# Sample attention in two visits a sample instead of three: the outputs are turned with the next sample's weights

## The chip, the cores and the metric

The kernel runs on one core of a Trainium2 chip. The metric is the device time of one execution in microseconds (us). The version before takes 2600.63 us, the median of 3 runs (2598.29 to 2601.8 us). One execution of it was profiled; it took 2600.23 us, and its span from the first to the last recorded instruction is 2598.4 us.

Engines are named as in the profile: PE is TensorE (matrix multiplications and transposes), PEld its weight loads, DVE is VectorE, ACT is ScalarE, POOL is GpSimd, SP is the engine whose queue issues most of the transfers. Each engine works through its own list of instructions in a fixed order; an instruction that waits holds up all that stand behind it in the same list.

## The reference

One inference step of a two-layer encoder over 512 prompt tokens and 8 running streams ("samples") of 16 new tokens, which share all weights. For each layer:

```
x += 1/2 * SwiGLU_1(RMSNorm(x))
z  = RMSNorm(x) @ w_in            # conv B | C | V | q | k | v | gates
y_c = B * causal_conv3(C * V)
y_a = attention(q, k, v)          # 8 heads of 64
m  = sigmoid(g_c) * (y_c @ w_conv_out) + sigmoid(g_a) * (y_a @ w_attn_out)
x += m @ w_o
x += 1/2 * SwiGLU_2(RMSNorm(x))
```

For a sample the attention has 16 queries, and 256 cached plus 16 new keys and values:

```
s   = q @ k_all.T / 8 + bias      # 8 heads x 16 queries = 128 rows, 272 columns
p   = softmax(s)
y_a = p @ v_all                   # a sum over 272 keys, for each head
```

Everything is computed in 32-bit floats; the large products are made of three matmuls with operands that are split into a high and a low part.

## The kernel before

All activations lie transposed, as tiles of 128 features by 640 tokens (512 of the prompt, then 16 for each sample). Weights come from memory in 384 blocks of 128 x 1024, issued from SP (`load`, line 204) into three buffers `raw`. ACT rounds each block to a high part `whi` (line 264), DVE subtracts it to get the low part `wlo` (line 269), each with three buffers; PE multiplies both.

The mixer's projections q, k, C, V, B and the gates are computed two output tiles at a time by `seven` (line 664): 14 *steps*, each a `block` (line 345) of six matmuls 128 x 320 into the PSUM tiles `ma`, `mb`, `mc`, with copies of partial sums (`capsm` and `c`, lines 681, 688, 691) between them. `others` and `qk` string these steps together into one `stream` of 140 steps a layer. `attention` (line 1103) interleaves the attention with it: `fill(n)` takes the next `n` steps of the stream, so that PE has something to do while ACT and DVE work on the softmax. The prompt's four pairs of heads take 68 of the steps, the eight samples the other 72, which are all that is left. What `fill` asks for beyond them gives PE nothing: only what follows the last step's matmuls on DVE and ACT is still put out then. The last steps of the stream are the first pair of gate tiles `g`, whose sigmoids (line 881) follow on ACT.

PE goes through its work in the order of the program (`manual_schedule(engines={PE})`, line 948). The order of DVE, ACT, POOL and SP within this part is set by a scheduler when the program is built, and the program then keeps to it. After `attention`, in `outputs` (line 1017), PE, DVE and ACT all follow the program's order. Its first work is `gate_pair(2)`, whose first matmuls go into the PSUM tile `qa`.

A sample `b` goes through these stages:

- `sscores(b)` (line 1257) issues the transfers of its cached keys (`kc`), cached values (`vc`) and new values (`vn`) from SP, and has POOL copy the new keys behind the cached ones. Four matmuls on PE make the scores `spss`; DVE adds the bias and writes them to a wide tile `ss` (called `box`), DVE and ACT make the softmax in it, without the division.
- `svalues(b)`, first part: PE turns the weights with three transposes (`sptp`, lines 1295 and 1296); ACT copies two of the results to `pt` (line 1298) and DVE the third to `pn` (line 1299), both further columns of the same `box`.
- second part: twelve matmuls make the outputs `spy` (line 1306); ACT scales them by the reciprocal of the sum and writes them to `yx` (line 1308), again columns of `box`.
- third part: PE turns `yx` with one transpose into its quarter of the PSUM tile `ptx` (line 1312), which four samples share. After the fourth, DVE and ACT copy `ptx` to `yas` (line 1317), which `outputs` reads later.

A *visit* is a place where PE leaves the stream for a sample. In the loop at line 1323 a sample has three: the weights' transposes; then the scores of sample `b + 2` with the outputs of sample `b`; then the output's transpose. With `fill` around them that is 4 steps, visit, 3 steps, visit, 2 steps, visit. PSUM has four banks for the tiles `spss`, `sptp`, `spy` and `ptx` (tag `att`), of which `ptx` holds one over four samples; the tiles of `outputs` take the same four banks after them. `box`, `vn` and `vc` have two buffers each (tags `pt`, `bias` and `s`), so what belongs to sample `b + 2` can be written only when the last reader of sample `b` is done.

## Time and profile before

| | before |
|---|---|
| median of 3 runs | 2600.63 us (2598.29 to 2601.8) |
| profiled execution | 2600.23 us |
| its span | 2598.4 us |
| PE busy | 2568.8 us, 99% |
| DVE busy | 1952.8 us, 75% |
| ACT busy | 1119.0 us, 43% |
| the sample section of the first layer | about 592 to 673 us of the span |
| the sample section of the second layer | about 1876 to 1956 us of the span |
| in 592 to 674 us: PE, DVE, ACT busy | 82.00, 65.22 and 40.30 of 82.00 us |
| one matmul 128 x 320 behind another | about 0.147 us from start to start |

Between the first and the last recorded instruction lie 2598.4 us; 1.8 us of the profiled execution lie around that. A row of a list in order of time has the start, the duration (of several instructions that are merged: from the first's start to the last's end), the engine, the line of the kernel, the operation, and what it writes and reads; "x8" says that eight instructions are merged, and a bracket at the end tells idle time before and what ended it. Matmuls overlap: one of 0.31 us starts 0.147 us after the one before it, so their cost is read from the distances of their starts. The fp32 matmuls of the samples stand twice in the records, a transpose once.

### The profile page before, as it was taken

The page shows a single profiled execution, that of the slowest core. Times are in us where ns is not written, and L with a number is a line of the kernel's source. Part 1 is how long each engine was busy: PE and PEld are TensorE (multiplying, and loading weights), DVE is VectorE, ACT ScalarE, POOL GpSimd, SP SyncE. Part 2 cuts the span into 40 slices and gives each one's busy share as a digit, 9 for nine tenths or more (in the row PEclk, how much of TensorE's full clock was granted, in tenths as well). Part 3 has the DMA queues.
Part 4 walks back from the last instruction along what each step waited for, and adds up shares of the span by engine and source line. Part 5 has one row for each costly group of instructions (what it writes and reads, how often), then busy time and mean ns, then how long its engine had stood idle before and what let it go on. Part 6 is the DMA issues. An engine that isn't in the chain of part 4 may idle for free.

```text
span 2598.4 us, 42553 instructions
## 1 busy us (share of the span) xinstructions
PE 2568.8 (99%) x17576; PEld 2506.6 (96%) x17576; DVE 1952.8 (75%) x3037; ACT 1119.0 (43%) x1738; POOL 59.6 (2%) x153
## 2 busy tenths in 40 slices
PE   8999999999999999999999999999999999999998
PEld 8999999888999999999999999998899999999998
DVE  7687768678777987767787767686876778877676
ACT  5343335454444543334454333355544445433332
POOL 0000000111000000000000000001110000000000
PEclk9999999999999999999999999999999999999999
DMA  3232222225222232222222222222342222222222
GB/s 132 72 106 84 74 90 98 98 88 165 97 74 90 67 104 82 73 90 81 82 82 98 74 90 82 76 98 101 119 145 89 82 82 79 91 91 74 87 90 76
DMA packets 74066, 237.06 MB, mean 91 GB/s; under 512 B 8240, under 2 KB 19120, under 8 KB 73872
## 3 DMA queue, kind: packets, MB, share of 16 engines
q1 hardware_dynamic: 70272, 223.90, 25.7%
q0 software_dynamic: 2880, 9.79, 1.1%
q8 instruction: 138, 2.26, 0.4%
q10 hardware_dynamic: 720, 0.65, 0.1%
q14 instruction: 56, 0.46, 0.1%
HBM read 225.85 MB, written 7.94 MB: 90 GB/s over the span
## 4 chain that ended last, share of the span: by engine, by line
PE 90%; DVE 6%; ACT 2%; issue 1%; DMA 1%; POOL 0%; SPq 0%; ACTq 0%; DVEq 0%; POOLq 0%
PE pab L351 12%; PE pda L337 11%; PE pdb L337 11%; PE paa L351 11%; PE pcb L351 6%; PE pca L351 5%; PE py L337 4%; PE po L337 4%; PE qa L351 4%; PE pbb L351 3%; PE pba L351 3%; PE pv L1156 2%; PE qc L351 2%; PE ma_cv L351 2%; DVE wlo L269 1%; PE ma_b L351 1%
## 5 line engine op out<-in xcount | busy, mean ns | idle before, releaser
L269 DVE TENSOR_TENSOR wlo<-raw,whi 128x1024 fp32r<-128x1024 f32 (+2 forms) x540 | 562.3, 1046 | 178.1 <-ACT whi L264 177.8
L264 ACT CAST whi<-raw 128x1024 fp32r<-128x1024 f32 (+2 forms) x540 | 490.4, 912 | 264.6 <-PE pca L351 79.4
L351 PE MATMUL pab<-xhib,whi 128*128 128x320 f32 x704 | 218.4, 310 | 0.4 <-ACT u_b L788 0.4
L351 PE MATMUL pab<-xlob,whi 128*128 128x320 f32 x704 | 217.5, 309 | 0.0
L351 PE MATMUL pab<-xhib,wlo 128*128 128x320 f32 x704 | 217.5, 309 | 0.0
L351 PE MATMUL paa<-xhia,whi 128*128 128x320 f32 x640 | 198.2, 310 | 0.7 <-ACT c_a L724 0.5
L351 PE MATMUL paa<-xloa,whi 128*128 128x320 f32 x640 | 197.7, 309 | 0.0
L351 PE MATMUL paa<-xhia,wlo 128*128 128x320 f32 x640 | 197.7, 309 | 0.0
L337 PE MATMUL pda<-ahia,whi 128*128 128x320 f32 x704 | 160.5, 309 | 0.6 <-DVE x L854 0.6
L337 PE MATMUL pda<-aloa,whi 128*128 128x320 f32 x704 | 160.5, 309 | 0.0
L337 PE MATMUL pda<-ahia,wlo 128*128 128x320 f32 x704 | 160.3, 309 | 0.0
L264 ACT CAST whi<-s 128x1024 fp32r<-128x1024 f32 (+1 forms) x120 | 109.5, 912 | 111.3 <-DVE s L208 89.5
L337 PE MATMUL pdb<-alob,whi 128*128 128x320 f32 x656 | 149.5, 309 | 0.0
L337 PE MATMUL pdb<-ahib,wlo 128*128 128x320 f32 x656 | 149.5, 309 | 0.0
L337 PE MATMUL pdb<-ahib,whi 128*128 128x320 f32 x656 | 149.3, 309 | 0.0
L269 DVE TENSOR_TENSOR wlo<-s,whi 128x1024 fp32r<-128x1024 f32 (+1 forms) x120 | 127.0, 1058 | 9.7 <-ACT whi L264 9.7
L351 PEld LDWEIGHTS pab<-xhib,whi 128*128 128x128 f32 x704 | 132.1, 188 | 1.2 <-ACT u_b L788 0.9
L351 PEld LDWEIGHTS pab<-xlob,whi 128*128 128x128 f32 x704 | 132.2, 188 | 0.2
L351 PEld LDWEIGHTS pab<-xhib,wlo 128*128 128x128 f32 x704 | 132.1, 188 | 0.0
L351 PEld LDWEIGHTS paa<-xhia,whi 128*128 128x128 f32 x640 | 120.2, 188 | 1.3 <-ACT c_a L724 0.8
L351 PEld LDWEIGHTS paa<-xloa,whi 128*128 128x128 f32 x640 | 120.2, 188 | 0.1
L351 PEld LDWEIGHTS paa<-xhia,wlo 128*128 128x128 f32 x640 | 120.2, 188 | 0.0
(576 smaller groups left out, 6965.0 us busy)
## 6 DMA issues: line engine op xcount, KB each, us to landing
raw<-in_wst SPq DMA_DIRECT2D x384, 512.0 KB, 3.5
kc<-in_kcache SPq DMA_DIRECT2D x32, 256.0 KB, 4.0
vc<-in_vcache SPq DMA_DIRECT2D x16, 512.0 KB, 4.6
bias<-in_pbias POOLq DMA_DIRECT2D x16, 256.0 KB, 3.1
x<-in_xin SPq DMA_DIRECT2D x8, 320.0 KB, 5.1
out_vo<-v POOLq DMA_DIRECT2D x10, 256.0 KB, 2.5
out_ko<-k POOLq DMA_DIRECT2D x8, 320.0 KB, 2.4
out_yout<-x SPq DMA_DIRECT2D x8, 192.0 KB, 1.9
```

The costliest lines, as they stand in the source:

```text
L264: ACT.copy(hi[:, d], src[:, c])
L269: DVE.tensor_tensor(out=lo, in0=src, in1=hi.bitcast(F32), op=ALU.subtract)
L337: PE.matmul(ps[:, a, :HT], w, x[:, a * HT : (a + 1) * HT], start=k == 0 and j == 0, stop=k == n - 1 and j == 2)
L351: PE.matmul(ps, a, b, start=start and kp == 0 and j == 0, stop=stop and kp == NP - 1 and j == 2, skip_group_check=True)
L1156: PE.matmul(pv[t], xx[:, t * P : (t + 1) * P], w[:, kk * AW : (kk + 1) * AW], start=c == 0 and kk == 0 and j == 0, stop=c == KT // 2 - 1 a ...
```

## The change

The output of sample `b` is no longer turned in a visit of its own. It waits until sample `b + 1` comes to the transposes of its weights, and is turned just ahead of them, in the same visit. A sample then has two visits: 5 steps of the stream, visit (one transpose for the sample before, three for this one), 4 steps, visit (scores of sample `b + 2`, outputs of sample `b`). The number of steps for a sample stays 9, and the instructions are the same; their places differ. The last sample's output has no next sample: it is turned behind the loop, after a `fill(2)`.

As `yx` now has to outlive the scores of sample `b + 2`, which take the buffer of `box`, it moves from `box` to the first 128 columns of the tile of the new values `vn`, which the output matmuls have read by then. That tile is allocated with all 128 rows in place of 16. `vn` of sample `b + 2` can now be loaded only when the output of sample `b` has been turned.

```diff
             rows = slice(b * TS, (b + 1) * TS)
-            vn = mp.tile([P, SEQ], F32, name=f"vn{n}", tag="bias")[:TS, :AW]
-            SP.dma_start(vn, vnew[rows])
+
+            vn = mp.tile([P, SEQ], F32, name=f"vn{n}", tag="bias")
+            SP.dma_start(vn[:TS, :AW], vnew[rows])
...
             pt = box[:, KS : KS + 2 * P].rearrange("p (a b) -> p a b", a=2)
-            pn, yx = (box[:n, KS + o * P : KS + (o + 1) * P] for n, o in ((TS, 2), (P, 3)))
+            pn = box[:TS, KS + 2 * P : KS + 3 * P]
+            yx, vn = vn[:, :P], vn[:TS]
...
         sscores(0)
         sscores(1)
+
+        vals = None
         for b in range(NB):
+            fill(5)
+            if vals:
+                next(vals, None)
             vals = svalues(b)
+            next(vals)
             fill(4)
-            next(vals)
-            fill(3)
             if b + 2 < NB:
                 sscores(b + 2)
             next(vals)
-            fill(2)
-            next(vals, None)
+        fill(2)
+        next(vals, None)
         fill(KT * KT)
```

## Prediction

> **What bounds the kernel now.** I read the page first (busy shares, chain), then the list of who waited for whom on PE, then the section in order of time on PE and ACT, then the granted clock by stretches.

> ```profile
> PE 2568.8 (99%) x17576; PEld 2506.6 (96%) x17576; DVE 1952.8 (75%) x3037; ACT 1119.0 (43%) x1738; POOL 59.6 (2%) x153
> ...
> PE 90%; DVE 6%; ACT 2%; issue 1%; DMA 1%; POOL 0%; SPq 0%; ACTq 0%; DVEq 0%; POOLq 0%
> ```

> PE is busy nearly all the time and carries 90% of the chain. A microsecond in which PE stands still is a microsecond of the kernel.

> ```profile
> PE ptp L1221 <- DVE s L1344: 10.1, 6, 2.3
> ...
> PE qa L351 <- ACT capsm L1043: 0.5, 2, 0.2
> ```

> PE's longest waits in the middle of the kernel are in the prompt's attention (ptp, up to 2.3 us). Asked for the sample section alone, this list is empty: PE waits there for nothing, so there is no wait that the change could remove. Just behind it, at line 1043 in each layer, comes a wait of 0.2 us.

> ```profile
> 666.40 0.31 PE L351 MATMUL ma_g<-tlo,whi 128*128 128x320 f32 x1
> 666.55 0.31 PE L351 MATMUL ma_g<-thi,wlo 128*128 128x320 f32 x1
> 666.70 0.38 PE L1295 MATMUL sptp<-ident,ss 128*128 128x128 f32 x2
> 666.91 0.27 PE L1296 MATMUL sptp<-ident,ss 128*16 128x128 f32 x1
> 666.94 0.39 PE L351 MATMUL ma_g<-thi,whi 128*128 128x320 f32 x1
> 667.17 0.31 PE L351 MATMUL ma_g<-tlo,whi 128*128 128x320 f32 x1
> ...
> 669.76 0.42 PE L1306 MATMUL spy<-vn,ss 16*32 16x128 f32 x8
> ...
> 672.41 0.31 PE L351 MATMUL ma_g<-thi,wlo 128*128 128x320 f32 x1
> 672.55 0.27 PE L1312 MATMUL ptx<-ident,ss 128*128 128x128 f32 x1
> 672.58 0.39 PE L351 MATMUL qa<-hhim,whi 128*128 128x320 f32 x1
> 672.81 0.31 PE L351 MATMUL qa<-hlom,whi 128*128 128x320 f32 x1
> ```

> This is the last sample of the first layer. The visit for the weights takes 666.55 to 667.17, 0.62 us, where two matmuls of the stream would take 0.29: 0.33 us for three transposes, 0.11 each. The visit for the output takes 672.41 to 672.81, 0.40 us against 0.29: 0.11 us for one. So a transpose costs the same alone or in company, and going to a visit costs nothing of its own.

> ```profile
> 671.04 0.36 ACT L1308 ACTIVATE ss<-spy,sst 128x128 f32<-128x128 f32 x1
> 671.43 0.62 ACT L264 CAST whi<-raw 128x512 fp32r<-128x512 f32 x1
> 672.08 1.28 ACT L881 ACT_TABLE_LOAD   x1
> 673.37 1.55 ACT L881 ACTIVATE g<-g,sm 128x640 f32<-128x640 f32 x2
> 674.94 0.37 ACT L1317 COPY ya<-ptx 64x256 f32<-64x256 f32 x1
> ```

> Same place on ACT: the last sample's scaling stands ahead of the table load and the two sigmoids of the gates, the copy of the turned outputs behind them.

> **The change part by part**, against the profiled execution's own 2600.23 us (0.4 below the median of the runs).

> *The visit that goes.* Eight samples, two layers: 16 transposes move from 0.11 us alone to 0.11 us in company. Taken from finer starts it is 0.003 us each, a gain of 0.05 us in all. Ends: 0 and 16 x 0.11 = 1.8, if the fourth transpose were free; the row of three at 0.11 each speaks for nearly 0.

> *More cover between the stages.* Weights' copies to output matmuls: 4 steps in place of 3 (one step is 0.88 us, half of "12 matmuls in 1.76"). Nothing waits there now, so this is worth 0.

> *The last sample, the costly part.* All 72 steps are used up when the loop ends, so the `fill(2)` behind it gives PE nothing, and the last transpose follows the last output matmuls directly. Those move behind the two steps that followed them: from 669.76 to 671.5, and PE comes to the transpose at about 672.45. But in the changed program's order of instructions the last scaling on ACT stands behind the weight cast, the table load and the first of the two sigmoids. By the rows above the first sigmoid begins at 673.37, the next instruction 0.74 later at 674.11; the scaling takes 0.36, so the transpose starts at 674.5: PE stands for 2.05 us. Then `qa`. Because `ptx` for samples 4 to 7 is now allocated after `spy` of sample 4, it gets the PSUM bank in which `qa` comes next (before, another), and the program's first `qa` matmul waits for ACT's copy of the turned outputs. ACT has the second sigmoid ahead of it (674.4, 0.74 apart), then the copy, 0.37: 675.5. `qa` began at 672.58, so 2.94 us later. The second layer has the same rows 1283.6 us later (table load at 1955.67): another 2.94. If ACT's list were no obstacle, the scaling alone (about 0.4 with its 0.28 us matmul latency ahead) would still be exposed: lower end about 0.7 a layer; upper end, both sigmoids and the copy one after another after 673.37, 3.2.

> *Behind it.* The wait at line 1043 (0.24 us at 680.12; the starts there are 0.55 apart instead of 0.15, so 0.40) comes from ACT being late with copies; ACT's list starts only 2.2 us later there and PE 2.9, so it goes: -0.40 a layer.

> *A new small wait in the first sample.* Behind its scaling the changed order on ACT has the cast of the next weights, the exponential of sample 2, then the partial sum `c`. PE's block that has to wait for this copy would start at 605.8. The cast can begin when the step before has been read, about 604.1, 0.95; exponential 0.52; copy 0.41: 606.0, and a restarted PE loses another 0.1 between the first two matmuls. 0.25 a layer (ends 0 and 0.4). I find no second place of this kind: elsewhere the copies are ready 0.3 us or more ahead.

> *SP.* `vn` now waits for the transpose of sample b, five steps later than the output matmuls, and the weight blocks stand behind it in SP's list. The tightest: one issued at 648.26 now stands behind a `vn` whose transpose comes at about 648.0 and whose issue takes 0.61: about 648.9, 0.6 late; what is made of it is needed 1.4 us or more after it is ready. 0, because of that cover; if none of the 16 were covered, 16 x 0.6 = 10.

> *The four copies to `yas`* move one visit on; DVE and ACT have room (65 and 40 of 82 us). 0.

> Sum a layer: 2.94 + 0.25 - 0.40 = 2.8, twice 5.6: **2605.8 us with PE at full clock.**

> *The clock after the stall.*

> ```profile
> 503.70:507.10 3.40, 2.98 (x21) 2.63 (x19) 3.40 (x9) 1.61 (x5) 1.22 (x3) 1.00 0.17 69
> 507.30:510.60 3.30, 1.52 (x8) 1.02 (x9) 3.24 (x9) 0.48 (x2) 0.00 (x0) 1.00 0.01 2
> 510.70:514.00 3.30, 3.30 (x15) 3.30 (x14) 1.77 (x2) 1.58 (x3) 0.00 (x0) 0.50 0.00 0
> 514.10:517.40 3.30, 3.30 (x24) 2.67 (x24) 1.61 (x4) 1.52 (x4) 0.00 (x0) 1.00 0.54 179
> ```

> The columns are the stretch, its length, PE busy with its count, PEld, DVE, ACT, POOL, then the granted clock. After a stretch with PE busy for 1.52 of 3.3 us (the 2.33 us wait at ptp) the clock is 0.50 for 3.4 us; the matmuls start 0.265 us apart instead of 0.147. That holds 13 instead of 23 and loses up to 1.5 us. It happens four times, after both such waits of each layer. The new stall is 2.9 us idle of 3.1. If a 3.4 us stretch holds most of it, the clock halves; if the boundary falls in its middle, perhaps not. I take 1.3 each (part of the half clock falls into the stall): 2605.8 + 2.6 = **2608.4 us**; ends 0 and 3.0.

> [...]

> **The rivals.**

> [...]

> *Not slower: `qa` does not wait for the copy.* If the stall ends with the transpose, as it would were the bank read out in time by the DVE half alone, a layer costs 2.05 + 0.25 - 0.40 = 1.9 and, with so much less idle time, no clock: 2604.0. It decides as soon as a layer loses under 2.6 us. Against: the program's wait is for ACT's half.

> *SP's list becomes the bound*: weight blocks come too late in the section. Where the 0.6 us delays exceed their cover in half the places, 16 x 0.6 / 2 = 5 on top: 2613. Against: the cover of 1.4 us.

> *Faster*: visits have a cost that the starts don't show. It would have to be over 0.35 us each, 16 times, to pay for the stall alone; the rows leave 0.003.

> **How the numbers follow.** Clock halved in both layers 0.42 (2608.4), in one 0.22 (2607.1), in none 0.17 (2605.8), no wait for the bank or a shorter stall 0.08 (2604.0), SP 0.08 (2613), faster 0.03. I predict 2608.4. The range 2604.5 to 2610.5 leaves out SP, faster and half of the short stall. A measurement of this kernel tells about 0.2%, 5.2 us, from no change: the border is 2605.8. Slower: nearly all of the first two, half of the third, SP: 0.78. Faster 0.03, within 0.19.

> **What would show it.** In the profile after: PE waiting about 2.05 us at ptx for ACT's line 1308 and 0.7 to 0.9 at `qa` for the copy to `ya`, once a layer; no waits elsewhere in the section except some 0.2 us at `mc_b` in the first sample; the wait at line 1043 gone; two more stretches of 0.50 clock behind `qa`. I am wrong if PE does not wait at the last ptx, if weight casts make it wait in mid-section, or if the clock stays at 1.00 behind `qa`.

## The result and the profile after

The changed kernel takes 2608.71 us, the median of 6 executions (2604.18 to 2611.66), beside 2600.22 us of the kernel before (6 executions, 2598.29 to 2601.8) on the same chip. The ratio is 1.0032, with a 95% interval of 1.0021 to 1.0044: slower. The profiled execution has a span of 2606.9 us, 8.5 us more than before.

The first view is again the list of who waited for whom on PE, in the kernel after (total us, times, longest us):

```profile
PE ptp L1221 <- DVE s L1350: 10.1, 6, 2.3
...
PE ptx L1314 <- ACT vn L1310: 3.8, 2, 1.9
PE qa L351 <- ACT ya L1319: 1.8, 2, 0.9
```

The prompt's waits at ptp are what they were. Two lines are new, once a layer each: PE waits 1.9 us at the last ptx for ACT's scaling, and 0.9 us at qa for ACT's copy to `ya`. The line of `capsm` at 1043 has left the list. Asked for the sample section without its end (590 to 672 us), the list is empty, as it was.

The end of the first layer's sample section in order of time, on PE:

```profile
671.36 0.42 PE L1308 MATMUL spy<-vn,ss 16*32 16x128 f32 x8
671.71 0.65 PE L1308 MATMUL spy<-vc,ss 128*32 128x128 f32 x16
674.24 0.33 PE L1314 MATMUL ptx<-ident,vn 128*128 128x128 f32 x1 [1.89 <-ACT vn L1310]
675.48 0.41 PE L351 MATMUL qa<-hhim,whi 128*128 128x320 f32 x1 [0.91 <-ACT ya L1319]
```

and the same stretch on ACT:

```profile
671.81 1.28 ACT L881 ACT_TABLE_LOAD   x1
673.11 0.83 ACT L881 ACTIVATE g<-g,sm 128x640 f32<-128x640 f32 x1
673.84 0.35 ACT L1310 ACTIVATE vn<-spy,sst 128x128 f32<-128x128 f32 x1
674.09 0.82 ACT L881 ACTIVATE g<-g,sm 128x640 f32<-128x640 f32 x1
675.06 0.37 ACT L1319 COPY ya<-ptx 64x256 f32<-64x256 f32 x1 [0.15 <-DVE ya L1319]
```

The outputs `spy` are done near 672.4, but ACT is in a table load and then in the first sigmoid; its scaling (line 1310) starts at 673.84, and PE follows at 674.24. The copy to `ya` starts at 675.06, and `qa` at 675.48. The bracket of the copy says that DVE's half of it ended last, 0.15 us after the second sigmoid.

Where the 8.5 us lie is read by setting the starts of the same matmuls in the two traces side by side, at places where both have the same visits behind them:

| what moves PE in the profiled execution | first layer | second layer |
|---|---|---|
| `mc_b` in the first sample | +0.37 | +0.37 |
| start of `qa`, from there | +3.00 | +3.03 |
| half clock behind `qa` | +1.55 | +1.39 |
| the wait at line 1043 and the restart behind it | -0.50 | -0.51 |
| sum | +4.42 | +4.28 |

At line 1043 the first matmul gains 0.41 and 0.42 us; the rest lies in the distance to the one behind it, which is 0.25 us after the wait and 0.15 without it. The table adds up to 8.7 us. The remaining -0.2 us are scattered: around the prompt's waits the first layer is 0.7 us faster than before and the second, which has one half-clock stretch more, 0.6 us slower; small drifts elsewhere make up the rest.

The granted clock behind the two stalls, by stretches of 3.41 us (length, busy time with count of PE, PEld, DVE, ACT and POOL, granted clock, DMA share, GB/s):

```profile
673.49:676.90 3.41, 1.75 (x10) 1.56 (x11) 1.01 (x2) 1.78 (x4) 0.00 (x0) 1.00 0.02 5
676.90:680.31 3.41, 3.41 (x15) 3.41 (x14) 0.91 (x1) 2.31 (x4) 0.00 (x0) 0.50 0.01 2
1960.31:1963.72 3.41, 0.96 (x21) 0.50 (x17) 2.78 (x6) 3.23 (x6) 0.00 (x0) 1.00 0.00 0
1963.72:1967.13 3.41, 3.05 (x11) 3.06 (x12) 0.00 (x0) 0.30 (x1) 0.00 (x0) 0.50 0.00 0
```

In both layers the stretch that follows runs at 0.50. The small wait in the first sample is seen on PE and on ACT:

```profile
605.16 0.31 PE L351 MATMUL ma_b<-thi,wlo 128*128 128x320 f32 x1
605.56 0.42 PE L351 MATMUL mc_b<-hhim,whi 128*128 128x320 f32 x1
605.82 0.31 PE L351 MATMUL mc_b<-hlom,whi 128*128 128x320 f32 x1
```

```profile
603.64 1.05 ACT L264 CAST whi<-raw 128x1024 fp32r<-128x1024 f32 x1 [0.57 <-PE mc_b L351]
604.59 0.52 ACT L1346 ACTIVATE ss<-ss,sst 128x272 f32<-128x272 f32 x1
...
605.11 0.40 ACT L691 COPY c<-mc_b 128x320 f32<-128x320 f32 x1
```

The block starts 0.40 us after the matmul before it, in place of 0.147, when the copy to `c` ends, which had the weight cast and sample 2's exponential ahead of it on ACT: 0.25 us. Its second matmul comes 0.26 later, another 0.11.

### The profile page after: what moved, and what is told of

Same layout as the page of the kernel before. It is cut to its first block, busy times and chain, and to the rows that moved or that the text cites. A ratio compares the mean times of both kernels' runs of the same rounds, so it can differ in the third digit from the quotient of the medians.

```text
span 2606.9 us, 42568 instructions
## 1 busy us (share of the span) xinstructions
PE 2572.3 (99%) x17576; PEld 2510.6 (96%) x17576; DVE 1953.2 (75%) x3037; ACT 1120.2 (43%) x1738; POOL 54.1 (2%) x153
## 4 chain that ended last, share of the span: by engine, by line
PE 90%; DVE 6%; ACT 2%; issue 1%; DMA 0%; POOL 0%; DVEq 0%; ACTq 0%; POOLq 0%
PE pab L351 12%; PE pda L337 11%; PE pdb L337 11%; PE paa L351 11%; PE pcb L351 6%; PE pca L351 5%; PE py L337 4%; PE po L337 4%; PE qa L351 4%; PE pbb L351 3%; PE pba L351 3%; PE pv L1156 2%; PE qc L351 2%; PE ma_cv L351 2%; DVE wlo L269 1%; PE mc_cv L351 1%
## 5 line engine op out<-in xcount | busy, mean ns | idle before, releaser
L264 ACT CAST whi<-raw 128x1024 fp32r<-128x1024 f32 (+2 forms) x540 | 490.7, 912 | 271.4 <-PE pca L351 79.4
L351 PE MATMUL pab<-xhib,whi 128*128 128x320 f32 x704 | 218.4, 310 | 0.4 <-ACT u_b L788 0.4
L351 PE MATMUL pab<-xlob,whi 128*128 128x320 f32 x704 | 217.5, 309 | 0.0
L351 PE MATMUL pab<-xhib,wlo 128*128 128x320 f32 x704 | 217.5, 309 | 0.0
L351 PE MATMUL paa<-xhia,whi 128*128 128x320 f32 x640 | 198.2, 310 | 0.7 <-ACT c_a L724 0.5
L351 PE MATMUL paa<-xloa,whi 128*128 128x320 f32 x640 | 197.6, 309 | 0.0
L351 PE MATMUL paa<-xhia,wlo 128*128 128x320 f32 x640 | 197.6, 309 | 0.0
L264 ACT CAST whi<-s 128x1024 fp32r<-128x1024 f32 (+1 forms) x120 | 109.5, 913 | 98.6 <-DVE s L208 80.6
L351 PEld LDWEIGHTS pab<-xhib,whi 128*128 128x128 f32 x704 | 132.1, 188 | 1.2 <-ACT u_b L788 0.9
L351 PEld LDWEIGHTS pab<-xlob,whi 128*128 128x128 f32 x704 | 132.2, 188 | 0.2
L351 PEld LDWEIGHTS pab<-xhib,wlo 128*128 128x128 f32 x704 | 132.1, 188 | 0.0
L351 PEld LDWEIGHTS paa<-xhia,whi 128*128 128x128 f32 x640 | 120.2, 188 | 1.3 <-ACT c_a L724 0.8
L351 PEld LDWEIGHTS paa<-xloa,whi 128*128 128x128 f32 x640 | 120.2, 188 | 0.1
L351 PEld LDWEIGHTS paa<-xhia,wlo 128*128 128x128 f32 x640 | 120.2, 188 | 0.0
```

The source lines that it names most:

```text
L264: ACT.copy(hi[:, d], src[:, c])
L351: PE.matmul(ps, a, b, start=start and kp == 0 and j == 0, stop=stop and kp == NP - 1 and j == 2, skip_group_check=True)
```

## The experiments

Times are medians, compared with executions of the kernel before on the same chip (medians 2600.03 to 2600.46 us). The theory under test: the loss is the end of the sample section (the missing steps in front of the last transpose, ACT's order, the PSUM bank) and the half clock behind it; the rest of the change costs nothing but 0.37 us a layer.

### Another bank for ptx

```diff
-            if vals:
-                next(vals, None)
-            vals = svalues(b)
-            next(vals)
+            old, vals = vals, svalues(b)
+            for v in (vals, old) if b == G + 1 else (old, vals):
+                if v:
+                    next(v, None)
```

> The changed kernel, with the PSUM bank of ptx for samples 4 to 7 and that of sptp for sample 5 exchanged (in one visit the weights are turned ahead of the outputs), so that qa gets a bank that was read out long ago; before 2600.2 us, changed 2608.7 us. If the wait of 0.91 us at qa comes from the bank alone, it goes in both layers and the wait of 1.9 us at ptx stays: 2606.9 us if the clock still halves behind the shorter stall, 2603.9 us if it does not. If qa waits for something else than the bank, nothing changes: 2608.7 us.

Measured: 2604.72 us, ratio 1.0019 (1.0009 to 1.0028). PE at the end of the first layer's section:

```profile
673.01 0.33 PE L1314 MATMUL ptx<-ident,vn 128*128 128x128 f32 x1 [1.89 <-ACT vn L1310]
673.09 0.39 PE L351 MATMUL qa<-hhim,whi 128*128 128x320 f32 x1
```

`qa` follows ptx at once: the 0.91 us are the bank's, in both layers, and the 1.89 us at ptx stay. In the profiled execution the clock is not halved behind either stall:

```profile
668.86:672.27 3.41, 2.25 (x34) 1.59 (x32) 3.41 (x8) 2.93 (x4) 0.00 (x0) 1.00 0.00 0
672.27:675.68 3.41, 2.67 (x19) 2.67 (x20) 0.99 (x2) 2.26 (x6) 0.00 (x0) 1.00 0.02 5
675.69:679.10 3.41, 3.41 (x25) 3.41 (x25) 2.50 (x3) 3.41 (x6) 0.00 (x0) 1.00 0.12 22
```

Here the idle time is split over two stretches. The execution that was profiled took 2600.32 us, which is less than the 2603.9 expected for a full clock and about what the kernel before takes, although both stalls are in it. Its prompt part explains that: there the trace has two half-clock stretches where the kernel before has four, and the starts show the two prompt parts 1.9 us and 1.8 us shorter. So the clock behind the prompt's waits differs from one trace to another too, and this profile is that of one of the fastest executions. The median lies between the two times expected for a full and a halved clock. Single executions spread from 2600.14 to 2608.39 us, at a mean granted clock of 0.997 in those below 2601 and 0.993 to 0.994 in the two above 2608.

### Two steps kept for the end

```diff
-            fill(5)
+            fill(5 - (b == NB - 1))
             if vals:
                 next(vals, None)
             vals = svalues(b)
             next(vals)
-            fill(4)
+            fill(4 - (b == NB - 1))
```

> The changed kernel, with one step taken from each of the last sample's two fills, so that the fill(2) behind the loop has two steps to give; the bank stays that of the changed kernel. My theory: the wait at ptx goes, since the scaling comes ahead of the table load on ACT again, but the copy to ya stays behind both sigmoids, and qa waits for it from about 672.3 to 675.4 instead: the whole stall moves to qa, about 2.8 us a layer, the clock halves as before, and the time is 2608.5 us (2606.5 to 2610). The rival, that the missing steps at ptx are the loss and the bank is only a detail on top: 2602 us or less.

Measured: 2607.92 us, ratio 1.0029 (1.0018 to 1.0041). The wait at ptx is gone, and the list of waits on PE has in its place:

```profile
PE qa L351 <- ACT ya L1319: 4.9, 2, 2.4
```

On ACT the scaling now comes ahead of the table load, and the copy still behind both sigmoids:

```profile
672.59 0.36 ACT L1310 ACTIVATE vn<-spy,sst 128x128 f32<-128x128 f32 x1
...
673.62 1.28 ACT L881 ACT_TABLE_LOAD   x1
674.92 1.55 ACT L881 ACTIVATE g<-g,sm 128x640 f32<-128x640 f32 x2
676.49 0.37 ACT L1319 COPY ya<-ptx 64x256 f32<-64x256 f32 x1
```

By the starts, with what the section had lost before taken off, `qa` comes 2.66 us later than before in each layer, where the theory had 2.8. With both causes it is 3.0 us, with the stall at ptx alone (the experiment above) 1.9. So each cause alone brings most of the delay, and they overlap. The rival, with 2602 us or less, falls.

The clock did not quite do as expected: in the profiled execution it is halved behind the wait in the second layer only.

```profile
672.40:675.81 3.41, 2.08 (x16) 1.80 (x13) 3.29 (x7) 3.35 (x6) 0.00 (x0) 1.00 0.00 0
675.82:679.23 3.41, 2.32 (x16) 2.32 (x17) 0.60 (x2) 1.22 (x3) 0.00 (x0) 1.00 0.02 5
1959.20:1962.61 3.41, 0.98 (x8) 0.71 (x6) 2.76 (x6) 3.27 (x5) 0.00 (x0) 1.00 0.00 0
1962.61:1966.02 3.41, 3.41 (x13) 3.41 (x14) 0.00 (x0) 0.00 (x0) 0.00 (x0) 0.50 0.00 0
```

In the first layer the idle time is split over two stretches. That this execution still took 2607.91 us is in part a coincidence: its trace is 1.4 us behind that of the kernel before from the first 11 us of the kernel on, far from the edit.

### Both edits together

The edits of the last two, in one kernel.

```diff
-            fill(5)
-            if vals:
-                next(vals, None)
-            vals = svalues(b)
-            next(vals)
-            fill(4)
+            fill(5 - (b == NB - 1))
+            old, vals = vals, svalues(b)
+            for v in (vals, old) if b == G + 1 else (old, vals):
+                if v:
+                    next(v, None)
+            fill(4 - (b == NB - 1))
```

> Both of the last two edits: two visits a sample, two steps behind the last outputs, and another bank for ptx. My theory: no stall at ptx, none at qa, no halved clock behind them, the wait of 0.2 us at line 1043 back; the rest of the change (visits in company, yx in the buffer of vn, later loads of vn on SP) costs nothing but the 0.37 us at mc_b in each layer's first sample: 2600.9 us (2600 to 2602). The rival, that merged visits or the delayed loads cost something in the section: over 2603 us. The rival that a visit has a price of its own: under 2599.5 us.

Measured: 2600.65 us, ratio 1.0003 (0.9995 to 1.0012). No wait is left at ptx or at qa:

```profile
672.22 0.27 PE L1314 MATMUL ptx<-ident,vn 128*128 128x128 f32 x1
672.25 0.39 PE L351 MATMUL qa<-hhim,whi 128*128 128x320 f32 x1
```

This kernel has two visits a sample, `yx` in the buffer of `vn`, and the later loads, and it is as fast as before; the interval leaves at most 3 us for all of that. Of the changes only the 0.37 us at `mc_b` are left in its trace, in each layer, and 0.1 us less at line 1043. The slowest of its 11 executions took 2602.25 us; that speaks against the rival of the delayed loads at over 2603 us; a price of 0.35 us for each visit, 5.6 us in all, would have shown as a gain.

### The stall alone, in the kernel before

```diff
         for b in range(NB):
             vals = svalues(b)
-            fill(4)
+            fill(4 + (b == NB - 1))
             next(vals)
-            fill(3)
+            fill(3 + (b == NB - 1))
```

> The kernel before, three visits a sample, yx in box, with nothing changed but the last sample: one step more in each of its first two fills, so that its fill(2) has none left. Of the change this is the last sample's missing cover alone, without the bank. My theory: ACT's order becomes that of the changed kernel (scaling behind the table load and the first sigmoid), PE waits 1.9 us at ptx and not at qa; qa 2.0 us later, 0.4 us less at line 1043, so 3.2 us in two layers: 2603.4 us with a full clock, 2606.3 us with the clock halved in both layers. The rival, that the loss comes from the visits or from yx in vn: 2600.2 us.

Measured: 2606.61 us, ratio 1.0028 (1.0017 to 1.0038). Three visits a sample, and still most of the loss: PE waits at ptx and not at qa.

```profile
PE ptx L1312 <- ACT ss L1308: 4.2, 2, 2.1
```

The profiled execution also has a wait of 0.8 us (1.0 by the starts) at `ma_cv` in the first layer's section, for a sum on DVE. DVE had stood 2.00 us for a weight block from memory shortly before; whether other executions have this wait is not known, and it belongs to no theory. The same stall of 2.1 us stands in both layers, and the clock tells them apart:

```profile
673.98:677.39 3.41, 1.84 (x13) 1.84 (x14) 1.82 (x4) 2.59 (x5) 0.00 (x0) 1.00 0.02 5
677.39:680.80 3.41, 3.41 (x25) 3.41 (x24) 1.71 (x2) 3.12 (x5) 0.00 (x0) 1.00 0.00 0
1957.39:1960.80 3.41, 1.38 (x28) 0.72 (x26) 3.32 (x6) 3.08 (x6) 0.00 (x0) 1.00 0.00 0
1960.80:1964.21 3.41, 3.34 (x13) 3.34 (x14) 0.42 (x1) 1.11 (x3) 0.00 (x0) 0.50 0.00 0
```

In the first layer PE was busy for 1.84 of 3.41 us and the clock stayed full; in the second for 1.38, and it was halved. So the 5.7 us by which this execution is behind the trace before are two stalls of about 2.15 us, less 0.5 each at line 1043, 1.4 us of clock in one layer, and the 1.0 us at `ma_cv`. That the median meets the 2606.3 expected for a clock halved in both layers is therefore in part luck.

### PE kept busy in the stall

```diff
+            for _ in range(16 if b == NB - 1 else 0):
+                PE.transpose(ptx[0][:, (b % G) * P : (b % G + 1) * P], ident, ident)
             PE.transpose(ptx[0][:, (b % G) * P : (b % G + 1) * P], yx, ident)
```

> The changed kernel with 16 more transposes of the identity, 0.11 us each, written just ahead of the last sample's transpose into the place that this one then overwrites. They fill some 1.76 of the 1.9 us for which PE stood at ptx; when PE goes on is unchanged, since ACT sets it: qa begins as late as in the changed kernel. If it is idle time that halves the clock, only 0.9 us of it are left, the clock stays full behind qa, and the time is that of the stalls alone, before plus two times 3.0: 2606.2 us, with no stretch of 0.50 behind qa in the profile. If the halved clock has another cause, or costs nothing, 2608.7 us as the changed kernel.

Measured: 2606.51 us, ratio 1.0023 (1.0014 to 1.0032), 2.2 below the changed kernel, near the 2606.2 of a full clock. In the profiled execution PE goes on when it did in the changed kernel, with 0.91 us of idle time left:

```profile
672.25 1.97 PE L1315 MATMUL ptx<-ident 128*128 128x128 f32 x16
674.22 0.33 PE L1316 MATMUL ptx<-ident,vn 128*128 128x128 f32 x1
675.45 0.41 PE L351 MATMUL qa<-hhim,whi 128*128 128x320 f32 x1 [0.91 <-ACT ya L1321]
```

and there is no half clock behind it in either layer, only the four stretches in the prompt part. The two kernels were not measured side by side, and their intervals overlap; this experiment's weight is in the trace, and the next one has the size.

### PE kept busy in the prompt's waits

```diff
                 ptp = att(f"ptp{l}_{2 * p + e}_{j}")[:, :w]
+                for _ in range(18 if p < 2 and j == 0 and e == 1 else 0):
+                    PE.transpose(ptp[:, :P], ident, ident)
```

> The kernel before, with 18 transposes of the identity (1.98 us) written ahead of the second head's first transposes in the prompt's first two pairs, where PE stands 2.3 us at ptp and the clock halves behind it, in both layers; nothing else changes, and the waits end when they did. If idle time halves the clock, the four half-clock stretches of 3.4 us go, at 1.5 us each (13 matmuls in place of 23): 2594.2 us (2593 to 2596). If they have another cause, 2600.2 us or, with the transposes in the way, up to 2602.

Measured: 2595.65 us, ratio 0.9981 (0.9972 to 0.9989). 72 useless transposes make the kernel before 4.8 us faster. The mean granted clock is 0.999, where it was 0.996:

```profile
core 0: 2594.1 us, clock 0.999
```

No half-clock stretch is left before the last 10 us. Expected were 6 us from the four stretches. The two prompt parts are 3.0 and 2.9 us shorter by the starts; part of it is given back further on (at two places the starts of `pab` lose 0.3 and 0.6 us again).

### Real work in the prompt's waits

The two visits free no time in the kernel as changed; this asks whether they free steps.

```diff
             scores(p)
-            fill(12)
+            fill(12 + 3 * (p < 2))
...
-            fill(5)
+            fill(4)
-            if vals:
-                next(vals, None)
-            vals = svalues(b)
-            next(vals)
+            old, vals = vals, svalues(b)
+            for v in (vals, old) if b == G + 1 else (old, vals):
+                if v:
+                    next(v, None)
             fill(4)
```

> A use for what the two visits free: in two visits a sample, with the other bank for ptx, eight steps a sample in place of nine (fill(4) in both places) and two behind the loop; the six steps saved in a layer go behind the scores of the prompt's first two pairs (fill(15) in place of 12), where PE stands 2.3 us at ptp for DVE. If the samples' stages are covered by four steps and four, and DVE has room for the three steps there, the waits at ptp go (9.7 us in all) with the half clocks behind them (6 us): 2586 us. If DVE, which the extra steps load too, comes later by as much, or the samples now wait, 2600 us or more. Between them if half of it remains: 2593 us.

Measured: 2584.52 us, ratio 0.9936 (0.9923 to 0.995): 15.9 us faster than before, 24.2 faster than the change.

```profile
PE ptp L1221 <- DVE s L1350: 2.0, 2, 1.0
PE pss L1197 <- DVE st L1200: 1.2, 2, 0.6
```

Of the 10.1 us at ptp 2.0 are left, 1.2 at `pss` are new, and the clock is full up to the last 10 us. That is 8.1 - 1.2 + 6 = 12.9 us. By the starts each layer is 8.3 to 8.4 us shorter from the prompt's attention to the first blocks of `outputs`, so the whole gain lies there. The 3 us or so that the sum lacks may be what PE loses when it starts again after a wait, which the list doesn't count; this is not itemised, and not shown.

### The same with three visits

```diff
             scores(p)
-            fill(12)
+            fill(12 + 3 * (p < 2))
...
-            ptp = att(f"sptp{n}")
+            ptp = early.get(b) or att(f"sptp{n}")
...
+            if b == G:
+                early[b + 1] = att(f"sptp{l}_{b + 1}")
+                PE.transpose(early[b + 1][:, :P], ident, ident)
             if b % G == 0:
                 ptx[0] = att(f"ptx{n}")
...
             vals = svalues(b)
-            fill(4)
+            fill(3 + 2 * (b == 0))
```

> The same move of six steps a layer to the prompt's first two pairs in the kernel before, with three visits a sample: fill(3), fill(3), fill(2) around a sample (five steps ahead of the first), and one extra transpose of 0.11 us in a layer that keeps ptx out of the bank of qa. Everything that stood between a sample's own stages stays; only the gap between its last visit and the next sample's weights is one step shorter. If the two visits are no condition for the gain, 2584.5 us as there, or 0.5 less without the wait at mc_b (2583 to 2586). If the third visit needs the ninth step, PE waits once a sample, and some of the 16 us stay away: 2590 us or more.

Measured: 2585.09 us, ratio 0.9943 (0.9929 to 0.9956). The two medians are 0.57 us apart, inside both intervals. The gain comes from where the steps stand, and three visits give it as well: the change is no condition for it.

## Why the prediction was right, and where it was off

*The last sample, the costly part.* Right in mechanism, place and order: ACT's list is the one foretold, and both waits are there. The term of 2.94 us measured 3.00 and 3.03. In absolute time `qa` came at 675.48, where the sum put it at 675.5; but PE's stream ran 0.1 us ahead of the sum's. ACT was ahead too, by 0.27 us, up to the second sigmoid; then the copy to `ya` had to wait 0.15 us for DVE's half, which was not in the sum. Of the wait at ptx the list shows 1.9 in place of 2.05, of that at `qa` 0.91 in place of 0.7 to 0.9.

*The bank.* The prediction added the bank's wait on top of the stall. The experiments show that the two are not terms of a sum: with the two steps kept back the bank's wait grows to 2.4 us, and without the bank the stall at ptx stays at 1.9. The sum came out because it went along ACT's list to its end, which sets both.

*Behind it.* -0.40 foretold, -0.50 and -0.51 measured. The prediction counted the late start (0.41 and 0.42) but not the longer distance to the matmul behind it, another 0.1, which it did count at `mc_b`.

*A new small wait in the first sample.* 0.25 foretold, 0.37 measured, with the two instructions named ahead of the copy; the end given was 0.4. The prediction's own figures (604.1 + 0.95 + 0.52 + 0.41, against 605.8) give 0.18 us of waiting and 0.1 for the restart, so 0.28 rather than 0.25; measured are 0.25 and 0.11. The wait is too short for the list and stands only in the starts.

*The visit that goes.* Four transposes in company cost 0.43 to 0.44 us by the starts after, 0.33 + 0.11 before: no gain. *SP:* the weight block foretold at about 648.9 was issued at 648.70, right behind a `vn`, and nobody waited for it. *More cover* and *the copies to `yas`*: nothing is seen of them.

*The clock after the stall.* Halved in both layers, as forecast, at 1.55 and 1.39 in place of 1.3 each. That both layers are halved is one outcome among several: somewhat shorter stalls of this kind (1.9 to 2.4 us) were followed by half clock in neither layer in the trace of "Another bank for ptx" and in one of two in "Two steps kept for the end" and "The stall alone". Nor does half clock always follow the prompt's four waits, as in the trace before: in the traces of "Another bank for ptx" and "Both edits together" only two of the four are followed by half clock. The reason given for it, that a 3.4 us stretch has to hold most of the stall, was an estimate, and it was close: half clock followed stretches with PE busy for 1.75 and 0.96 of 3.41 us. The last section has the other stretches.

*The rivals.* A full clock behind the stalls of both layers, which had a chance of 0.17, happened in the experiment with PE kept busy, not in the profiled execution of the change. "qa does not wait for the copy" is out (0.91 us, twice). For SP and the faster case the kernel with both edits leaves no room: 2600.65 us.

The terms add up to 8.7 in the trace against 8.2 in the prediction (0.1 more at the stalls, 0.2 at `mc_b`, 0.3 for the clock, 0.2 less at line 1043), and 0.2 us of scatter elsewhere bring the profiled execution to 8.5. That the median came within 0.3 us is partly luck, since single executions spread over 7.5 us, and the mean granted clock with them (0.997 in the fastest, 0.993 in the slowest).

## What to carry to other kernels

Before merging or moving a stage, ask what covers its last instance: in a loop that feeds on a finite stock of filler work, the last round has none, and there the order of another engine's list (here a table load of 1.28 us and two activations of 0.83 ahead of a copy of 0.37) stands in the open. A wait that is removed there may only move to the next resource that the same list releases, here the PSUM bank (1.9 us at ptx became 2.4 at `qa`), so change both before you judge. Here a stall of 1.9 and 0.9 us on PE cost more than itself, by 1.55 and 1.39 us of half clock behind it, and whether half clock followed stalls of about two microseconds changed from one trace to another: look at the granted clock behind each wait, in more than one trace, and move filler work there from where it is not needed.

## What the runs showed of the hardware

Not tried: another order on ACT at the end (the scaling ahead of the table load with the steps as the change has them), and what would take the 0.37 us at `mc_b` away.
